# Counts loaded by twelves, rows fetched in 2 KB pieces, and nested fourth parts with jump hints in a two-layer mixture-of-experts kernel

## The chip, the cores and the metric

The kernel runs on one core of a Trainium2 chip. The metric is the device time of one execution in microseconds. Five engines work beside each other: TensorE (PE, with its weight loads as PEld), VectorE (DVE), ScalarE (ACT), GpSimd (POOL) and SyncE (SP). Here SP issues the transfers of weights, and POOL issues the gathers and scatters of token rows. Each engine runs its own instruction stream; semaphores order them. PE's stream also holds jumps, and loads of counts into its registers.

## The reference, cut to what matters

Two layers, each a token mixer and then a grouped top-2 mixture of 16 experts; layer 0 has 512 tokens (context and latent), layer 1 has 256. The part that the change touches:

```python
def moe_ffn(h, idx, w, w_gate, w_up, w_down):
    flat_e = idx.reshape(-1)
    order = jnp.argsort(flat_e)
    ...
    def expert_block(args):
        xb, ei = args
        return (jax.nn.silu(xb @ w_gate[ei]) * (xb @ w_up[ei])) @ w_down[ei]
    ...
    y = yb[dest] * w.reshape(-1)[order][:, None].astype(h.dtype)
    return jnp.zeros_like(h).at[tok].add(y)
```

`D_MODEL` is 1024, `D_EXPERT` 768. How many tokens go to an expert is known only at run time.

## The kernel before, in words

Each layer's expert stage (`moe`) goes through the 16 experts e in eight pairs p, with m = 0 or 1 for the expert of the pair. SP brings every weight once: four pieces `in_egu` (gate and up) and two `in_ed` (down) of 1536 KB for each expert, into a ring of slots that PE frees as it goes on (`wload`). A pair's tokens are gathered by POOL (`gather`, L1561, tile `xg`) and transposed on PE (`xt`).

An expert's tokens lie in a window of 128 (layer 0) or 96 (layer 1), cut in parts of 32. `hidden` computes gate and up for each part t into a PSUM tile `gu`, ACT and DVE make `sg` and `h` of it; `down` multiplies with the down weights into `dp`, with S = 0 for parts 0 and 1 and S = 1 for parts 2 and 3. A part's matmuls are 32 in gate and up and 24 in down; in f32 each of these is two weight loads and two matmuls on PE, so a part of gate and up is 128 instructions. In layer 0 parts 2 and 3, and in layer 1 parts 1 and 2, run only if the expert's count n exceeds 32 t: `when` (L1483) puts a run-time branch (L1487) around the part, and one matmul with a zero tile fills PSUM if it is left out. In layer 0 the third and the fourth part stand behind two branches, one after the other, in gate/up and in down.

The counts come from a tile `cnt` (`counts`, L1404): 16 of the experts, 8 maxima of the pairs, one overall. PE loads each into a register by itself (`count`, L1737): a TENSOR_LOAD and two check instructions, 31 times a layer. POOL loads those it needs in the same way (L1557, L1602).

In layer 0 the outputs of pairs 0 to 5 go by `scatter` to four planes in DRAM, a quarter of the columns each; S = 1 is sent only if the pair's maximum exceeds 64. A send is four indirect DMAs, one for each plane. After the last, `fetch(a)` brings half of the tokens back: 16 DMAs of 128 KB, then two POOL additions (L1615) of the two choices of each token. `collect` (tile `cl`) transposes the sum on PE and adds it to the result: half 0 at the end of expert 13, half 1 at the end of expert 14. The last two pairs are added by matmuls with one-hot tiles (`combine`, `cm`).

PE's expert matmuls keep the order in which the program writes them (`pin`); the work around them is placed by a scheduler.

## Time and profile before

| | |
|---|---|
| median of 3 runs | 1477.56 us (1477.24 to 1483.76) |
| profiled execution | 1479.13 us |
| its span in the trace | 1477.4 us |
| PE busy | 1250.3 us, 85% of the span |
| DVE, ACT, POOL busy | 682.2, 398.0, 140.8 us |
| DMA | 411.87 MB, mean 279 GB/s |
| mean granted clock of PE | 0.921 |

The page gives the mean over stages with different limits. Layer 0's expert stage lies from 391 to about 850 us, layer 1's from 1088 to about 1454. To read it, one takes the stages apart: where the DMA share is near one, the weights set the time; where PE is neither busy nor waiting for weights, its waits are to be looked up. "issue" in a wait means that nothing in the profile explains it; branches, register loads and checks are not counted as busy, and the waits that they cause appear in this way or under PEq, PE's sequencer.

### The profile page before, as it was taken

Reading aid. Unit: us, or ns where it says so; the run is one execution under the profiler, and the core shown is the slowest. Engines: PE = TensorE matmul, PEld = TensorE weight load, DVE = VectorE, ACT = ScalarE, POOL = GpSimd, SP = SyncE. Lnnn points to the kernel's source line nnn. Section 1 sums busy time; section 2 is a strip of 40 time slices with the busy share of each in tenths; the row PEclk is TensorE's granted clock in tenths of the full one; section 3 lists DMA queues with packets and bytes.
Section 4 is the critical chain, followed back from the end, with each engine's and each line's share of the span. In section 5 each row is a group of like instructions: output and inputs, shape, how many; then the busy total and the mean of one; then the engine's idle time right before and its main releaser. Section 6 shows DMA issues by size and latency. Waiting matters only on the chain. (4 is left out here: it accounts for less than half of the span.)

```text
span 1477.4 us, 27647 instructions
## 1 busy us (share of the span) xinstructions
PE 1250.3 (85%) x11433; PEld 726.9 (49%) x11434; DVE 682.2 (46%) x1773; ACT 398.0 (27%) x791; POOL 140.8 (10%) x153
## 2 busy tenths in 40 slices
PE   4999988898679799999878867998978688898774
PEld 0697553576334344554434435876833344454333
DVE  1847536876425111111123568737665245454445
ACT  2624234344110110111010134434431112121214
POOL 0000011102101111022133012002010000000000
PEclk8999999899799999999989988999989898998996
DMA  9421688134488998889998341273388999999981
GB/s 359 163 100 43 223 323 343 52 128 161 178 338 315 382 412 369 347 329 421 426 386 341 144 160 55 89 278 150 129 340 360 377 412 425 423 426 421 425 367 31
DMA packets 49475, 411.87 MB, mean 279 GB/s; under 512 B 7195, under 2 KB 11439, under 8 KB 18064
## 3 DMA queue, kind: packets, MB, share of 16 engines
q1 hardware_dynamic: 41200, 388.40, 64.6%
q0 software_dynamic: 7232, 17.71, 3.3%
q8 instruction: 140, 2.29, 0.6%
q10 hardware_dynamic: 864, 3.15, 0.5%
q14 instruction: 39, 0.32, 0.1%
HBM read 402.02 MB, written 13.11 MB: 281 GB/s over the span
## 5 line engine op out<-in xcount | busy, mean ns | idle before, releaser
L1665 DVE SCALAR_TENSOR_TENSOR h0p<-gu0p,gt0p,sg0p 128x192 f32<-128x192 f32 x64 | 25.3, 415 | 177.0 <-ACT sg0p L321 176.5
L345 PE MATMUL gu0p<-big,xe0p 128*32 128x384 f32 x992 | 91.8, 492 | 1.6 <-issue 1.4
L345 PE MATMUL gu1p<-more,big 128*32 128x384 f32 x976 | 85.5, 493 | 7.9 <-issue 3.0
L321 ACT ACTIVATE sg0p<-gu0p 128x192 f32<-128x192 f32 x64 | 19.6, 331 | 247.1 <-PE gu0p L345 243.8
L345 PE MATMUL gu0p<-ring,xe0p 128*32 128x384 f32 x768 | 74.8, 497 | 0.8 <-ACT sg0p L321 0.5
L345 PE MATMUL gu0p<-more,xe0p 128*32 128x384 f32 x800 | 74.7, 493 | 0.5 <-issue 0.5
L345 PE MATMUL ada<-ring,small 128*32 128x512 f32 x344 | 62.9, 684 | 14.2 <-DMA ring<-in_ada 14.2
L1665 DVE SCALAR_TENSOR_TENSOR h1p<-gu1p,gt1p,sg1p 128x192 f32<-128x192 f32 x48 | 19.9, 415 | 118.0 <-ACT sg1p L321 117.9
L345 PE MATMUL dp0p<-big,hT0p 128*32 128x256 f32 x792 | 59.4, 402 | 6.3 <-issue 4.0
L345 PEld LDWEIGHTS gu1p<-more,big 128*32 128x32 f32 x976 | 35.1, 111 | 51.3 <-issue 46.1
L345 PEld LDWEIGHTS gu0p<-big,xe0p 128*32 128x32 f32 x992 | 37.8, 111 | 45.4 <-issue 42.1
L321 ACT ACTIVATE y0p<-dp0p 64x512 f32<-64x512 f32 (+1 forms) x40 | 23.6, 591 | 132.9 <-PE dp0p L345 105.0
L321 ACT ACTIVATE y1p<-dp1p 64x512 fp32r<-64x512 f32 x64 | 37.9, 592 | 79.9 <-PE dp1p L345 79.1
L321 ACT ACTIVATE sg1p<-gu1p 128x192 f32<-128x192 f32 x48 | 15.9, 330 | 156.4 <-PE gu1p L345 141.0
L321 ACT ACTIVATE big<-big 128x512 f32<-128x512 f32 (+2 forms) x81 | 44.7, 575 | 48.8 <-DVE big L641 21.5
L1598 POOL DMA_INDIRECT plane<-y0p,to0p x36 | 35.6, 988 | 205.8 <-ACT y0p L321 180.0
L345 PE MATMUL zo<-zo,zw 128*128 128x256 f32 x384 | 54.7, 292 | 0.0
L345 PE MATMUL gu1p<-big 128*32 128x384 f32 x528 | 52.5, 510 | 0.0
L345 PE MATMUL dp0p<-ring,hT0p 128*32 128x256 f32 x624 | 48.9, 401 | 3.5 <-issue 3.2
L345 PEld LDWEIGHTS zo<-zo,zw 128*128 128x128 f32 x384 | 48.6, 191 | 6.6 <-issue 4.3
L345 PEld LDWEIGHTS <-zero 128*128 128x128 bf16 x105 | 10.0, 97 | 83.2 <-issue 64.8
L1730 DVE TENSOR_TENSOR y1p<-dp1p,y1p 64x512 fp32r<-64x512 f32 x64 | 44.0, 688 | 5.5 <-ACT y1p L321 3.9
(558 smaller groups left out, 2425.2 us busy)
## 6 DMA issues: line engine op xcount, KB each, us to landing
more<-in_egu SPq DMA_DIRECT2D x54, 1536.0 KB, 15.3
big<-in_egu SPq DMA_DIRECT2D x48, 1536.0 KB, 15.6
ring<-in_ada SPq DMA_DIRECT2D x27, 1536.0 KB, 8.0
ring<-in_ed SPq DMA_DIRECT2D x27, 1536.0 KB, 14.8
ring<-in_egu SPq DMA_DIRECT2D x26, 1536.0 KB, 13.5
big<-in_ed SPq DMA_DIRECT2D x21, 1536.0 KB, 12.9
more<-in_ed SPq DMA_DIRECT2D x16, 1536.0 KB, 10.7
ring<-in_odw SPq DMA_DIRECT2D x5, 1536.0 KB, 6.2
```

What stands on the lines that cost most here:

```text
L321: a = self.nc.scalar.activation(out, x, func, **kw)
L345: i = self.nc.tensor.matmul(out, lhsT, rhs, start=start, stop=stop, skip_group_check=True)
L1598: nc.gpsimd.indirect_dma_start(out=self.planes[q], out_offset=bass.IndirectOffsetOnAxis(ap=to[:, q, i, S:S + 1], axis=0), in_=Y[S][:, q // ...
L1665: nc.vector.scalar_tensor_tensor(H[:, t], p[:, 192:384], gt[:, 2 * m + t % 2, i, t // 2:t // 2 + 1], sg, op0=OP.mult, op1=OP.mult)
L1730: nc.vector.tensor_tensor(yl[r, q], dp[r], yh[r, q].bitcast(F32), op=OP.subtract)
```

## The change

`counts` puts the numbers of a pair and their maximum next to each other. PE loads twelve registers (four pairs) with one instruction, without checks, at the stage's start and again ahead of expert 6. There are two planes of twice the length instead of four: a plane holds half of the columns, a token's two quarters lie one behind the other, so a row index is 2 to + (q mod 2), and `fetch` brings four DMAs of 512 KB in pieces of 2 KB instead of sixteen of 128 KB. The scatters go in the order q = 0, 2, 1, 3, which alternates between the planes. Half 1 is collected in expert 15, behind its parts 0 and 1. Parts 2 and 3 of layer 0 (the third and the fourth) stand in one branch (n > 64), the fourth nested in the third behind a branch of its own (n > 96), and the PSUM tiles of both are taken ahead of it. A hint that the jump is likely taken stands in PE's stream some matmuls ahead of the branches on n > 64, for every expert. The diff, cut to its core:

```diff
     def open_planes(self, pool):
...
-        self.planes = [self.dram.tile([2 * T, 256], F32, name=f'plane{q}') for q in range(4)]
+        self.planes = [self.dram.tile([4 * T, 256], F32, name=f'plane{q}') for q in range(2)]
...
-        nc.vector.tensor_copy(cf[:, :NE], count)
...
+        c3 = cf[:, :3 * NP].rearrange('p (q x) -> p q x', x=3)
+        nc.vector.tensor_copy(c3[:, :, 0:2], count.rearrange('p (q m) -> p q m', m=2))
+        nc.vector.tensor_reduce(c3[:, :, 2], c3[:, :, 0:2], axis=AX.X, op=OP.max)
...
-        def when(rv, least, yes, no=None):
+        def when(rv, least, yes, no=None, label=None):
...
-            with tc.If(rv > least) as cmp:
+            with tc.If(rv > least, label=label) as cmp:
...
+        def hint(rv, label):
+            if rv is not None:
+                with tc.issue_after(self.last):
+                    tc.mark_branch_hint_location(label, hint=0, engines=[mybir.EngineType.PE])
...
-                        nc.vector.tensor_copy(to[r, q], tg[s, 2])
+                        nc.vector.tensor_scalar(to[r, q], tg[s, 2], 2.0, q % 2 * 1.0, op0=OP.mult, op1=OP.add)
...
-                for q in range(4):
-                    nc.gpsimd.indirect_dma_start(out=self.planes[q], out_offset=bass.IndirectOffsetOnAxis(ap=to[:, q, i, S:S + 1], axis=0),
+                for q in (0, 2, 1, 3):
+                    nc.gpsimd.indirect_dma_start(out=self.planes[q // 2], out_offset=bass.IndirectOffsetOnAxis(ap=to[:, q, i, S:S + 1], axis=0),
...
-                for i in range(2):
-                    for q in range(4):
-                        o = i * T + a * TC + j * 128
-                        nc.gpsimd.dma_start(rb[:, j, i, q * 256:(q + 1) * 256], self.planes[q][o:o + 128])
+                for q in range(2):
+                    o = a * TC + j * 128
+                    nc.gpsimd.dma_start(rb[:, j, :, q * 512:q * 512 + 512],
+                                        self.planes[q].rearrange('(i t c) d -> t i (c d)', i=2, c=2)[o:o + 128])
...
-            def part(t, j=range(4)):
-                p = self.ps(f'gu{l}{nm}{t}', 'pj' if m or t < 2 else 'b')
-                when(rv if t > l_first else None, 32 * t, lambda: [gu_mm(t, jj, p) for jj in j], lambda: z_mm(p, 384))
-                return p
...
+            def third():
+                part(2)
+                if nt > 3:
+                    when(rv, 96, lambda: part(3), lambda: zeros(3))
...
                     if j == 1:
+                        hint(rv, f'gu{l}{nm}')
                         middle()
...
             between()
+            p += [self.ps(f'gu{l}{nm}{t}', 'pj' if m else 'b') for t in range(2, nt)]
+            when(rv, 64, third, lambda: [zeros(t) for t in range(2, nt)], f'gu{l}{nm}')
             for t in range(2, nt):
-                swiglu(t, part(t))
+                swiglu(t, p[t])
...
+                def third():
+                    if nt > 3:
+                        when(rv, 96, lambda: d_mm(1), lambda: z_mm(dp, 512))
+                    else:
+                        z_mm(dp, 512)
+                    d_mm(0)
                 if S == 0:
+                    hint(rv, f'dp{l}{nm}')
...
-                    when(rv, 64, lambda: d_mm(0))
+                    when(rv, 64, third, lambda: z_mm(dp, 512), f'dp{l}{nm}')
...
+        def some_counts(e):
+            i = 3 * (e // 2)
+            _, n = nc.values_load_multi_w_load_instructions(cnt[0:1, i:i + 3 * NC // 2], engines=[mybir.EngineType.PE], min_val=0, max_val=T,
+                                                                skip_runtime_bounds_check_because='counts of T tokens, compared with constants only')
+            for p in range(NC // 2):
+                ns_[e + 2 * p], ns_[e + 2 * p + 1], ns_[NE + e // 2 + p] = n[3 * p:3 * p + 3]
+
         def count(i):
-            return nc.tensor.value_load(cnt[0:1, i:i + 1], min_val=0, max_val=T)
+            return ns_[i]
+        ns_, NC = {}, 8
...
         for e in range(NE):
             p, m = divmod(e, 2)
+            if e == NC - 2:
+                with tc.issue_after(self.last):
+                    some_counts(NC)
...
+                if ns and e == 2 * ns + 3:
+                    collect(got, 1)
...
-            if ns and 1 <= e - 2 * ns <= 2:
-                collect(got, e - 2 * ns - 1)
-                if e == 2 * ns + 1:
-                    got = fetch(1)
+            if ns and e == 2 * ns + 1:
+                collect(got, 0)
+                got = fetch(1)
```

PE before, an expert of layer 0 behind its parts 0 and 1 (the rows `gu0p_4346` and `gu0p_4347` are those two, `ISA x2` are the checks of a count):

```order
L1737 TENSOR_LOAD cnt_2917
L1737 ISA x2
L1737 TENSOR_LOAD cnt_2917
L1737 ISA x2
L1487 COMPARE_AND_BRANCH
L345 MATMUL gu0p_4421<-more_2060,xe0p_4183 32x384 x16
L345 MATMUL gu0p_4421<-big,xe0p_4183 32x384 x8
L345 MATMUL gu0p_4421<-ring,xe0p_4183 32x384 x8
L1487 UNCONDITIONAL_BRANCH
L345 LDWEIGHTS zero_2776
L345 MATMUL gu0p_4421<-zero_2776 128x384
L1487 UNCONDITIONAL_BRANCH
```

PE now, the same place (`gu0p_4929` and `gu0p_4930` are parts 0 and 1, `gu0p_5005` the third, `gu0p_5006` the fourth):

```order
L1874 BRANCH_PREFETCH_HINT
L345 MATMUL gu0p_4929<-ring,xe0p_4744 32x384 x8
L345 MATMUL gu0p_4930<-ring,xe0p_4744 32x384 x8
L1489 COMPARE_AND_BRANCH
L345 MATMUL gu0p_5005<-big,xe0p_4757 32x384
L1489 COMPARE_AND_BRANCH
L345 MATMUL gu0p_5006<-big,xe0p_4757 32x384 x8
L345 MATMUL gu0p_5006<-ring,xe0p_4757 32x384 x16
L345 MATMUL gu0p_5006<-big,xe0p_4757 32x384 x8
L1489 UNCONDITIONAL_BRANCH
L345 LDWEIGHTS zero_2772
L345 MATMUL gu0p_5006<-zero_2772 128x384
```

The loads between the matmuls are gone, a hint stands two groups of matmuls ahead, and the first jump now spans the third part with the branch of the fourth inside it.

POOL before, a send of a pair, with the gather of the pair after next (`xg`) behind S = 0; a DMASW semaphore is the landing of a DMA that POOL issued earlier:

```order
L1598 DMA plane_1413<-y0p_4199,to0p_3091 1024x256 [waits DMASW0_49,DMASW2_49,DVE_49,Activation_49]
L1598 DMA plane_1414<-y0p_4199,to0p_3091 1024x256 [waits DMASW3_49,DMASW1_49]
L1598 DMA plane_1411<-y0p_4199,to0p_3091 1024x256 [waits DMASW4_49,DVE_49]
L1598 DMA plane_1412<-y0p_4199,to0p_3091 1024x256 [waits DMASW7_49,DMASW5_49]
L1561 DMA xg_2061<-rows_2063,idx0p_3601 128x1024 [waits DMASW6_49,PE_49]
L1603 COMPARE_AND_BRANCH
L1598 DMA plane_1411<-y0p_4200,to0p_3091 1024x256 [waits DMASW2_49]
L1598 DMA plane_1412<-y0p_4200,to0p_3091 1024x256 [waits DMASW3_49]
```

POOL now, the same send:

```order
L1606 DMA plane_1412<-y0p_4160,to0p_3095 2048x256 [waits DMASW6_49,DMASW2_49,DMASW7_49,DVE_49,Activation_49]
L1606 DMA plane_1411<-y0p_4160,to0p_3095 2048x256 [waits DMASW3_49,DVE_49]
L1606 DMA plane_1412<-y0p_4160,to0p_3095 2048x256 [waits DMASW6_49]
L1606 DMA plane_1411<-y0p_4160,to0p_3095 2048x256 [waits DMASW7_49]
L1611 COMPARE_AND_BRANCH
L1606 DMA plane_1411<-y0p_4161,to0p_3095 2048x256 [waits DMASW1_49]
L1606 DMA plane_1412<-y0p_4161,to0p_3095 2048x256 [waits DMASW0_49]
L1606 DMA plane_1411<-y0p_4161,to0p_3095 2048x256 [waits DMASW4_49,DMASW2_49]
```

The third scatter waits for the landing of the first, since both write one plane, and the gather stands behind the second send instead of ahead of it.

PE before, the collect of half 1 between expert 14's down matmuls and expert 15's first gate and up matmuls:

```order
L345 MATMUL dp0p_7758<-big,hT0p_7641 32x256 x12
L350 MATMUL cl_7867<-const,rows_7564 128x128 x4
L350 MATMUL cl_7874<-const,rows_7564 128x128 x4
L350 MATMUL cl_7881<-const,rows_7564 128x128 x4
L350 MATMUL cl_7888<-const,rows_7564 128x128 x4
L345 MATMUL gu0p_7910<-big,xe0p_7394 32x384 x8
L345 MATMUL gu0p_7911<-big,xe0p_7394 32x384 x8
```

PE now, the end of expert 15's parts 0 and 1:

```order
L345 MATMUL gu0p_7683<-more_2056,xe0p_7228 32x384 x8
L345 MATMUL gu0p_7684<-more_2056,xe0p_7228 32x384 x8
L351 MATMUL cl_7759<-const,rows_7400 128x128 x4
L351 MATMUL cl_7766<-const,rows_7400 128x128 x4
L1489 COMPARE_AND_BRANCH
L345 MATMUL gu0p_7854<-big,xe0p_7241 32x384
```

The transposes of `cl` stand behind the two parts, ahead of the branch on the third. At the start of layer 0's expert stage POOL has eight single count loads ahead of its first gather, where it had four.

## Rows read from the trace of the kernel before

**Rows 1.** Stretches: length, busy PE, PEld, DVE, ACT, POOL, clock, DMA share, GB/s.

```profile
600.00:700.00 100.00, 95.50 (x1297) 48.32 (x1289) 15.78 (x28) 12.41 (x30) 17.42 (x18) 1.00 0.91 375
...
752.00:815.00 63.00, 48.37 (x536) 23.40 (x536) 19.58 (x40) 7.65 (x18) 20.66 (x26) 0.86 0.89 351
...
1088.00:1180.00 92.00, 70.04 (x718) 36.88 (x717) 40.74 (x199) 17.21 (x36) 2.12 (x2) 0.89 0.85 347
1180.00:1440.00 260.00, 218.77 (x2462) 108.41 (x2461) 120.42 (x411) 53.43 (x107) 5.94 (x6) 0.91 0.99 415
```

**Rows 2.** Waits of PE from 752 to 815: us in total, times, longest.

```profile
PE cl L350 <- POOL rows L1615: 13.0, 2, 8.2
```

**Rows 3.** Timeline of POOL from 733 to 800: start, length, instruction, idle before it.

```profile
733.84 0.98 POOL L1598 DMA_INDIRECT plane<-y0p,to0p  x1 [32.02 <-ACT y0p L321]
...
750.46 4.22 POOL L1613 DMA_DIRECT2D rows<-plane  x8 [0.95 <-DMA rows<-plane]
...
766.62 2.34 POOL L1615 TENSOR_TENSOR rows<-rows 128x1024 f32<-128x1024 f32 x1 [9.54 <-issue]
775.22 4.29 POOL L1613 DMA_DIRECT2D rows<-plane  x8 [6.25 <-PE cl L350]
```

**Rows 4.** Timeline of PE from 752 to 815.

```profile
769.01 2.61 PE L350 MATMUL cl<-const,rows 128*128 128x128 f32 x11 [8.21 <-POOL rows L1615]
...
798.90 3.46 PE L350 MATMUL cl<-const,rows 128*128 128x128 f32 x15 [4.76 <-POOL rows L1615]
802.29 6.40 PE L345 MATMUL gu0p<-big,xe0p 128*32 128x384 f32 x64
```

**Rows 5.** Line L1598 (scatter) from 730 to 770.

```profile
DMA to landing us min/median/max: 6.6/7.5/7.8
```

**Rows 6.** Waits of PE from 391 to 752.

```profile
PE gu0p L345 <- issue: 10.2, 7, 5.0
PE xt0p L350 <- DMA xg<-rows,idx0p: 6.0, 1, 6.0
PE gu0p L345 <- DVE h0p L1665: 4.9, 6, 1.1
```

**Rows 7.** Line L1487 (jumps), 391 to 856: durations ns min/median/max.

```profile
L1487 PEldq COMPARE_BRANCH  x98: 65/208/5807, 393.1 to 847.0; - x98
```

**Rows 8.** Reads of the zero tile from 391 to 856, same columns.

```profile
L345 PE MATMUL gu0p<-zero x24: 322/336/501, 402.3 to 816.0; 128*128 128x384 bf16 x24
L345 PE MATMUL dp0p<-zero x14: 376/390/391, 429.5 to 833.3; 128*128 128x512 bf16 x14
```

**Rows 9.** Timeline of PE around jumps and count loads.

```profile
441.25 0.50 PE L345 MATMUL gu0p<-zero 128*128 128x384 bf16 x1 [5.01 <-issue]
...
486.77 0.59 PE L345 MATMUL xt0p<-zero 128*128 128x512 bf16 x2 [1.46 <-ACT sg0p L321]
...
508.77 0.34 PE L345 MATMUL gu0p<-zero 128*128 128x384 bf16 x1 [0.90 <-issue]
511.07 0.50 PE L345 MATMUL gu0p<-zero 128*128 128x384 bf16 x1 [1.96 <-issue]
...
677.78 0.38 PE L345 MATMUL dp0p<-zero 128*128 128x512 bf16 x1 [1.71 <-issue]
```

**Rows 10.** Line L1737 (count loads) on PE from 440 to 860.

```profile
L1737 PEldq TENSOR_LOAD <-cnt x15: 297/300/319, 485.0 to 507.8; - x15
```

**Rows 11.** Line L1557 (count loads of POOL), and the timeline from 380.

```profile
L1557 POOLq TENSOR_LOAD <-cnt x15: 281/289/830, 382.4 to 1099.7; - x15
...
386.68 1.14 POOL L1561 DMA_INDIRECT xg<-rows,idx0p  x1 [14.29 <-DVE sp0p L1535]
```

**Rows 12.** Stretches in which the DMA engines stand in layer 1.

```profile
1100.50:1106.00 5.50, 5.50 (x46) 1.73 (x49) 5.03 (x40) 2.37 (x3) 0.00 (x0) 1.00 0.06 19
1124.50:1127.50 3.00, 2.35 (x31) 1.74 (x24) 0.91 (x3) 0.66 (x2) 0.00 (x0) 1.00 0.00 0
```

**Rows 13.** DMA issues of SP from 735 to 815.

```profile
751.90 0.33 SPq L338 DMA_DIRECT2D ring<-in_ed  x1
```

More of the change, by code (lines that the diff above doesn't have):

```diff
@@ L345, in mm @@
         i = self.nc.tensor.matmul(out, lhsT, rhs, start=start, stop=stop, skip_group_check=True)
+        self.last = i.ins
         if self.pin:
@@ L1681, in hidden @@
                     if j == 1:
+                        hint(rv, f'gu{l}{nm}')
                         middle()
@@ L1748, in gathers @@
             for S in range(2):
-                gather(info[p][0][0], info[p][1], S, NE + p)
+                gather(info[p][0][0], info[p][1], S, p)
         xe, G0 = [], []
@@ L1800, in experts @@
                         got = fetch(0)
-            if ns and 1 <= e - 2 * ns <= 2:
-                collect(got, e - 2 * ns - 1)
-                if e == 2 * ns + 1:
-                    got = fetch(1)
-            last, was = [f'p{p}{m}', m, (f'p{p}{m}', H), rv], (tok, ti, full, to, i, NE + p)
+            if ns and e == 2 * ns + 1:
+                collect(got, 0)
+                got = fetch(1)
+            last, was = [f'p{p}{m}', m, (f'p{p}{m}', H), rv], (tok, ti, full, to, i, p)
             if e == 1 and l == 0:
@@ L1814, in experts @@
             self.pin = pin
-        most = nc.values_load(cnt[0:1, NE + NP:NE + NP + 1], min_val=0, max_val=T)
+        most = nc.values_load(cnt[0:1, 3 * NP:3 * NP + 1], min_val=0, max_val=T)
         with tc.If(most > WIN[l]):
```

44 lines of the change are left out of this document (22 added, 22 removed).

## The prediction

> **What bounds the kernel now.** I read the span by stages first, in the table of stretches [rows 1]: it gives for each the busy time of TensorE (PE) and the share of the DMA engines. It shows three regimes. In layer 0's expert stage before 752 us both are nearly full: in 600 to 700, PE is busy 95.50 of 100 us and the DMA share is 0.91. There the weights and the matmuls wait for each other in turn, so a microsecond taken off PE returns in part. From 752 to 815 PE is busy for only 48.37 of 63 us. In layer 1 from 1180 to 1440 the DMA share is 0.99: the weights set the time there, and nothing that PE gains can show before the last of them lands.
>
> The waits of PE in 752 to 815 name what is late: 13.0 us in two waits for the POOL additions of L1615 [rows 2]. PE's timeline puts them at 769.01 (8.21 us) and 798.90 (4.76 us) [rows 4]. The weights were not late there: the second wait stands ahead of matmuls that then run without one, at 802.29. So these 13.0 us are the largest single item that a change in this code can take, and they lie on the path to layer 0's end. The other PE gaps of this stage are smaller and scattered: jumps over skipped thirds and fourths (L1487), and the count loads (L1737).
>
> **The change part by part.** *Fetch and collect.* POOL's timeline [rows 3] shows the chain: the four scatters of the last pair start at 733.84, one behind the other; sixteen fetch DMAs go out in two eights, the second from 750.46 over 4.22 us; the second addition starts at 766.62, so its data were late, not POOL. SP had issued 1536 KB weight pieces at 751.90 and after [rows 13], level with the second eight, and shares the engines with it.
>
> Now the third scatter writes the plane of the first and waits for its landing, 7.5 us in the median [rows 5]. It goes out near 733.8 + 7.5 = 741.3, the fourth near 742.6, and they land near 750. Four fetches are issued then, at the 0.53 us of one of the eight (4.22 / 8), so by about 752.5: 2 us before the last of the sixteen, and ahead of or level with SP's burst rather than behind it. The bytes are the same 2 MB. Lower end: they get through before the burst, the additions (2.34 us) end by 760.5, and 8.21 us vanish. Upper end: they share with the burst as before, and 8.21 remain. I take the half, 4.2 gained.
>
> The second collect moves from the end of expert 14 to behind the first two parts of expert 15. Before, its chain took from the fetch at 775.22 to PE's start at 798.90, 23.7 us; it starts now about 4 us earlier and has four issues instead of sixteen, while PE comes to it later by those two parts (the 64 rows from 802.29, half of them, alone are 6.40 us [rows 4]). So it is ready with some 10 us in hand, and 4.76 us go. Sum: -9.0, ends -4.8 and -13.0. What is late next is PE itself.
>
> *Counts on PE.* A single load is 0.300 us in the median [rows 10], with two check rows behind it, and 31 a layer become two loads of twelve. The trace exposes 1.46 us at 486.77 and 0.90 at 508.77 behind such loads [rows 9]; all of PE's waits that nothing in the profile explains ahead of gate/up matmuls are 10.2 us, 7.0 of which are two jumps (below) [rows 6], so the loads cost 2.4 to 4.7 us; I take 3.5. The first twelve loads cost nothing, since PE waited 6.0 us for the first gathered rows beside them [rows 6]. What one load of twelve costs no row shows: 0.30 if it is one access, 3.6 if it is twelve. The first stands directly behind PE's first gate/up matmul, the second behind 36 queued down matmuls, which hide a part. I take 2.0 and 1.0, so -0.5 net; ends -4.4 and +4.8.
>
> [...]
>
> *Counts on POOL.* POOL still loads singly, and eight such loads stand ahead of the first gather now, four before. One is 0.289 us plus its two checks, so four add 1.2 us and up to about twice that; the gather of before started at 386.68, held by VectorE [rows 11], and that wait hides a part. PE waits for this gather, so what is left counts in full: I take 0.9 (ends 0 and 2.4). Both count parts together: +0.4.
>
> *Jumps.* The zero fills of layer 0 say how often they are taken [rows 8]: 14 experts fill the down result (no fourth part), so 2 run it; 24 gate/up fills leave 10 experts that skip the third part as well. These 10 skip 256 instructions in one jump now, where they took two jumps over 128, and 192 where it was twice 96 in the down part: 20 long jumps. A jump is 0.208 us in the median but 5.807 at worst [rows 7], and the worst stood between two zero fills, exactly where the second jump goes: PE idled 5.01 us at 441.25; 1.96 at 511.07 is the same place of another expert, 1.71 at 677.78 a down part [rows 9]. That is 8.7 us; with smaller ones of 0.3 to 0.5 us I count 10 for layer 0. No row shows a hint at work in this place, so it is bounded: all 10 returned, or none with more lost (a rival). I take half, -5, since some of it only turns into waiting for weights. Against it stands that the PSUM tiles of both parts are taken ahead of the jump: in six places PE already waits for VectorE's h0p (4.9 us [rows 6]) ahead of the third part, and will wait for the second h0p too, some 0.4 us each, +2.5. Net -2.5; ends -10 and +8.
>
> *Scatters earlier in layer 0.* The same landing wait holds POOL some 6 us more for each send, and for a pair with over 64 rows the next gather now stands behind both sends. Gathers are issued while the pair before still runs, and PE waited for gathered rows only once, at the start [rows 6], so I cost this at nothing; if that cover went, it would be some 6 us for each such pair.
>
> *Layer 1.* Loads and jumps go there too, but only in 1088 to 1180 does the DMA share (0.85) leave room [rows 1]. In 1124.5 to 1127.5 it is 0.00 with PE busy 2.35 of 3 us [rows 12]: such holes, where SP waits for slots that PE has yet to free, are all that can return. In the longest, 1100.5 to 1106, PE is full, so only work ahead of it could shorten it. I take -2; ends 0 and -6, of the 8.5 us of the two.
>
> **Sum.** -9.0 + 0.4 - 2.5 - 2 = -13.1 us. The profiled execution was 1479.1 us (span 1477.4), 1.6 above the median of 1477.6 that the measurement will use; the terms are differences, so from the median the forecast is 1464.5.
>
> **The rivals.** *The first wait stays and the hints do nothing.* POOL's serial scatters put the fetches level with SP's burst, and the jumps still miss. For it: the 7.5 us landing [rows 5] is certain, and the margin over the burst is under 2 us. Then only 4.8 us of the second wait and a little else go: about 1473, within the bound of no change.
>
> *The long jumps miss.* Place: the 20 long jumps of layer 0, PE-bound before 752. [...] Price: if each exposed the 1.96 us of 511.07, 39 us come in and the 10 of today go: 1477.6 - 9 + 0.4 + 2.5 - 2 + 29 = 1498.5. It decides from about 1.0 us per long jump above what I assumed ((13.1 + 7.4) / 20). Against it: before, two jumps skipped the same code, with a matmul between, and only some missed.
>
> [...]
>
> *More comes back.* Both POOL waits vanish (-13), jumps and loads return all (-10, -4), and layer 1's holes close (-6), less 3.4 for the gather and the second h0p: about 1448. For it: the items are all real idle time of PE; against it: before 752 the DMA share is 0.9.
>
> **How the numbers follow.** Forecast (1457 to 1470): 0.45. More comes back (1444 to 1457): 0.21. First wait stays (1470 to 1481): 0.23. Long jumps miss: 0.11, part of it still under 1485. The bound of 0.5% (7.4 us) is about what a measurement of this kernel tells from no change, so faster means under 1470.2, slower over 1485: 0.66, 0.25, 0.09. The range 1448 to 1481 leaves out the far ends of both outer cases.
>
> **What would show it.** Right: no wait of PE for the POOL additions at the second collect, at most 4 us at the first; POOL's third scatter idle for some 6 us behind the first's landing; no PE gap of 5 us between zero fills in layer 0; TENSOR_LOAD on PE in four rows in all; layer 1's 1180 to 1440 unchanged at a DMA share of 0.99. Wrong: COMPARE_BRANCH rows of 1 us and more at many of the long jumps, a load of twelve well over 3.6 us, or a first collect as late as before.

## The result, and the profile after

The changed kernel takes 1494.51 us in the median of 8 runs (1490.74 to 1499.29), beside 1479.09 us of the kernel before: the ratio is 1.0095 with a 95% interval of 1.0077 to 1.0114. It is slower, by about 14 us. The forecast was 1464.5 with a range of 1448 to 1481: wrong in sign, and outside the range.

In the differences of ratios below, 0.001 is 1.48 us; a difference of two such ratios is good to about 4 us.

**Where the time came in.** The first PE row of layer 1's preparation (tile `adat`) is a landmark: what stands before it is layer 0. PE's timeline of the kernel before, then of the kernel after (start, length, instruction, idle before it):

```profile
855.60 0.65 PE L350 MATMUL adat<-const,adarow 128*128 128x128 f32 x4 [0.72 <-ACT adarow L435]
```

```profile
872.40 0.66 PE L351 MATMUL adat<-const,adarow 128*128 128x128 f32 x4 [0.68 <-ACT adarow L436]
```

Layer 0 ends 16.8 us later. From there to the end of the span it was 1477.4 - 855.6 = 621.8 us and is 1493.3 - 872.4 = 620.9. All that was lost was lost in layer 0. The stretch of layer 1 in the kernel after answers [rows 1]: the weights set the time there as before, at a DMA share of one.

```profile
1180.00:1440.00 260.00, 213.10 (x2376) 99.75 (x2380) 115.80 (x396) 53.25 (x106) 5.92 (x6) 0.89 1.01 425
```

**First place: the lists.** Among shorter stretches of layer 0 in the same view, one stands out. Of the kernel before:

```profile
445.00:470.00 25.00, 25.00 (x290) 12.93 (x286) 10.88 (x19) 1.80 (x5) 0.00 (x0) 0.98 0.90 371
```

Of the kernel after:

```profile
445.00:470.00 25.00, 15.58 (x74) 12.03 (x71) 11.52 (x31) 0.59 (x1) 1.00 (x1) 0.50 0.53 223
```

PE was busy 25.00 of 25 us with 290 matmuls, and is busy 15.58 with 74; the granted clock fell from 0.98 to 0.50, and the DMA share from 0.90 to 0.53. PE's timeline of the kernel after says with what:

```profile
445.92 1.02 PE L345 MATMUL sl0p<-aux,G0p 128*128 128x10 f32 x4
448.52 1.02 PE L345 MATMUL sl0p<-aux,G0p 128*128 128x10 f32 x4 [1.58 <-DVE G0p L1521]
...
466.52 1.02 PE L345 MATMUL sl0p<-aux,G0p 128*128 128x10 f32 x4 [0.78 <-DVE G0p L1521]
467.47 4.71 PE L345 MATMUL gu0p<-ring,xe0p 128*32 128x384 f32 x32
```

Twelve groups of four small matmuls (`sl0p`, the token lists of pairs 2 to 7; each group reads a tile `G0p` that DVE makes just ahead of it) stand in one block. Eleven of them wait for DVE, 1.58 + 10 x 0.78 = 9.4 us, and the gate/up matmuls behind them start at a low clock: 4.71 us for the 32 of 467.47, at 0.58 from 467.5 to 472.2, where 32 take 2.76 us at 1.00 (the row at 706.78 below). Nothing in the diff names these lists. The order of instructions shows how they moved. PE before, in this place (rows of the order, not of the trace):

```
L345 MATMUL sl0p_3528<-aux_2778,G0p_3529 128x10 x4
L345 MATMUL gu0p_3705<-ring,xe0p_3392 32x384 x7
L345 MATMUL gu0p_3706<-ring,xe0p_3392 32x384 x8
L345 MATMUL gu0p_3705<-more_2060,xe0p_3392 32x384
L345 MATMUL sl0p_3528<-aux_2778,G0p_3535 128x10 x4
L345 MATMUL gu0p_3705<-more_2060,xe0p_3392 32x384 x7
```

PE now:

```
L345 MATMUL dp0p_3412<-big,hT0p_3263 32x256 x15
L345 MATMUL sl0p_3519<-aux_2774,G0p_3520 128x10 x4
L345 MATMUL sl0p_3519<-aux_2774,G0p_3526 128x10 x4
L345 MATMUL sl0p_3519<-aux_2774,G0p_3532 128x10 x4
```

`mm` ties each matmul of an expert behind whatever was written on PE just before it. Before, that was a count load, which is itself tied to nothing, so expert 2's gate/up matmuls could be placed between the lists, and while DVE made the next `G0p`, PE had work. Now the count loads of expert 2 are gone, and its first matmul is tied behind the last list.

**Second place: the fetch.** POOL's timeline of the kernel after, which answers [rows 3]:

```profile
744.83 0.99 POOL L1606 DMA_INDIRECT plane<-y0p,to0p  x1 [16.85 <-ACT y0p L321]
...
751.23 0.98 POOL L1606 DMA_INDIRECT plane<-y0p,to0p  x1 [4.11 <-DMA plane<-y0p,to0p]
753.70 0.98 POOL L1606 DMA_INDIRECT plane<-y0p,to0p  x1 [1.49 <-DMA plane<-y0p,to0p]
760.16 2.99 POOL L1620 DMA_DIRECT2D rows<-plane  x4 [5.48 <-DMA plane<-y0p,to0p]
776.11 2.33 POOL L1623 TENSOR_TENSOR rows<-rows 128x1024 f32<-128x1024 f32 x1 [12.96 <-DMA rows<-plane]
786.19 2.34 POOL L1623 TENSOR_TENSOR rows<-rows 128x1024 f32<-128x1024 f32 x1 [7.75 <-DMA rows<-plane]
```

SP's DMA issues in the kernel after, which answer [rows 13] (1536 KB each):

```profile
757.45 0.33 SPq L338 DMA_DIRECT2D ring<-in_ed  x1
758.74 0.33 SPq L338 DMA_DIRECT2D big<-in_ed  x1
760.03 1.62 SPq L338 DMA_DIRECT2D big<-in_egu  x2
767.91 0.33 SPq L338 DMA_DIRECT2D ring<-in_egu  x1
771.16 0.33 SPq L338 DMA_DIRECT2D more<-in_egu  x1
```

And PE's timeline of the kernel after at the collect, which answers [rows 4]:

```profile
778.49 0.47 PE L351 MATMUL cl<-const,rows 128*128 128x128 f32 x1 [7.39 <-POOL rows L1623]
788.58 2.61 PE L351 MATMUL cl<-const,rows 128*128 128x128 f32 x11 [9.61 <-POOL rows L1623]
```

The third and the fourth scatter now wait for the landing of an earlier one, and the four fetches go out from 760.16, in the midst of a burst of six weight pieces. 2 MB of rows share the engines with 9 MB of weights, at a DMA share of 1.01 from 757.45 to 786.19, and the second addition starts 26 us after the first fetch was issued. PE waits 7.39 + 9.61 = 17.0 us for the first collect, where it waited 13.0 for both [rows 2]. At the second collect (828.34 and after) it waits for no addition, as was forecast.

**The smaller things.** Lines of the loads and the hint in the kernel after (durations ns min/median/max):

```profile
L1760 PEldq TENSOR_LOAD <-cnt x4: 850/871/1030, 398.5 to 1236.6; - x4
```

```profile
L1874 PEldq BRANCH_PREFETCH_HINT  x53: 31/31/50, 422.8 to 1454.2; - x53
```

Waits of PE from 391 to 756 in the kernel after, which answer [rows 6] (us in total, times, longest):

```profile
PE dp0p L345 <- issue: 15.0, 6, 3.7
PE sl0p L345 <- DVE G0p L1521: 10.2, 12, 1.6
PE xt0p L351 <- DMA xg<-rows,idx0p: 9.0, 1, 9.0
PE gu0p L345 <- issue: 7.2, 3, 3.7
```

A load of twelve takes 0.87 us. The waits that nothing explains, where the jumps show, are 15.0 + 7.2 = 22.2 us; before, up to 752, they were 11.6 (for `dp0p`) + 10.2 [rows 6] = 21.8. The wait for the first gathered rows grew from 6.0 to 9.0 us.

### The profile page after: what moved, and what is told of

Same layout as the page of the kernel before. It is cut to its first block, busy times and chain, and to the rows that moved or that the text cites. A ratio compares the mean times of both kernels' runs of the same rounds, so it can differ in the third digit from the quotient of the medians.

```text
span 1493.3 us, 27443 instructions
## 1 busy us (share of the span) xinstructions
PE 1245.8 (83%) x11433; PEld 738.3 (49%) x11434; DVE 683.0 (46%) x1773; ACT 398.9 (27%) x791; POOL 127.4 (9%) x127
## 5 line engine op out<-in xcount | busy, mean ns | idle before, releaser
L345 PE MATMUL gu0p<-ring,xe0p 128*32 128x384 f32 x768 | 80.8, 515 | 0.0
L345 PE MATMUL gu0p<-more,xe0p 128*32 128x384 f32 x800 | 71.6, 486 | 0.0
L345 PEld LDWEIGHTS gu0p<-big,xe0p 128*32 128x32 f32 x992 | 44.9, 110 | 36.4 <-issue 25.8
L345 PE MATMUL gu1p<-big 128*32 128x384 f32 x528 | 57.0, 548 | 3.8 <-DMA big<-in_egu 2.8
```

Source lines behind the costliest of these rows:

```text
L345: i = self.nc.tensor.matmul(out, lhsT, rhs, start=start, stop=stop, skip_group_check=True)
```

## The experiments

Every kernel below computes everything. Names beginning with a are the kernel after with something undone, with b the kernel before with something of the change done alone; c, d and e are combinations.

**Is it the lists?** a_spread takes away only the tie between the last list and expert 2's first gate/up matmul; the rest of the change stays.

```diff
-        if self.pin:
+        if self.pin and not self.loose:
             self.tc.keep_in_program_order(i)
+        self.loose = False
...
             W = load_gu(e)
+            self.loose = l == 0 and e == 2
```

> The changed kernel, but expert 2's first gate/up matmul of layer 0 is not pinned behind the token lists of pairs 2 to 7, so that the list matmuls can lie between the expert matmuls again, as they did before the change. Theory (removing the single count loads removed the breaks in PE's pinned order, and the twelve list matmul groups became one block, in which PE idled 9.4 us in eleven waits for G0p): about 9 us below the changed kernel's 1494.5, so 1484 to 1488, and no row of 0.78 us waits between 446 and 466. Rival (the weights set the time there and PE's waits in the block cost nothing): 1492 to 1496.

Measured: 1478.11 us, ratio 1.0003 (0.9985 to 1.0021), 13.6 us less than the kernel after. The stretch of a_spread:

```profile
445.00:470.00 25.00, 25.00 (x240) 12.15 (x239) 9.60 (x16) 1.81 (x5) 0.00 (x0) 0.86 1.01 428
```

PE's timeline of a_spread, two lists with expert 2's work between:

```profile
455.52 0.61 PE L347 MATMUL sl0p<-aux,G0p 128*128 128x10 f32 x4
456.06 1.50 PE L347 MATMUL gu0p<-more,xe0p 128*32 128x384 f32 x16
457.48 0.61 PE L347 MATMUL sl0p<-aux,G0p 128*128 128x10 f32 x4
```

All list groups but the first cost 0.61 us instead of 1.02 with 0.78 of waiting. The gain is 4 us more than the 9.4 us of waits, which fits the lists in the block and the matmuls behind them running at the granted clocks of 0.50 and 0.58 read above. b_block is the counterpart, the kernel before with the lists forced into one block:

```diff
+            if self.block is not None:
+                self.tc.add_manual_dep(i.ins, self.block.name, NOSYNC)
```

> The kernel before with one edit to the order alone: expert 2's matmuls in layer 0 are queued behind the twelve list groups, so that these stand in one block as in the changed kernel; every load, jump and DMA stays. Theory (the block is the main cause of the loss: 9.4 us of waits for G0p, some 5 us more for the same list matmuls and what follows at half the granted clock): 10 to 14 us more, 1.007 to 1.0095 of before, with a granted clock near 0.5 in the block. Rival (the lists only cost together with the changed loads and hints): 0.998 to 1.003.

Measured: 1489.42 us, 1.0072 (1.0050 to 1.0093), 10.6 us lost by the order alone. Its stretch:

```profile
445.00:470.00 25.00, 15.14 (x110) 12.12 (x106) 9.89 (x18) 0.59 (x1) 0.00 (x0) 0.64 0.33 129
```

So the block costs 10.6 to 13.6 us, shown from both sides. Of what the change lost against the kernel before, it is the largest part.

**Is it the first gather?** a_gate issues POOL's count loads behind the first gather.

```diff
+        def after_gate(load):
+            if l:
+                return load()
+            with tc.issue_after(self.gate):
+                return load()
```

> The changed kernel, but POOL's count loads are issued behind the first gather of layer 0 instead of ahead of it. Theory (eight single loads hold the gather, and PE waits for it): the gather starts at least 3 us earlier against the end of the router's work, and the time is 2 to 5 us below 1494.5, so 1489.5 to 1492.5. Rival (the gather was held by VectorE's list entries all the same): no change, 1494 to 1495.

Measured: 1489.47 us, 1.0086 (1.0060 to 1.0112). PE's wait for the first gather is 5.9 us again instead of 9.0; the time is 1.3 us less, less than can be told apart.

**Is it the planes, the hints or the nesting?** a_nohint leaves out the hints, a_flat_nohint the nesting as well; a_planes goes back to four planes, their scatter order and sixteen fetches.

```diff
-            if rv is not None:
+            if False:
                 with tc.issue_after(self.last):
                     tc.mark_branch_hint_location(label, hint=0, engines=[mybir.EngineType.PE])
```

> The changed kernel without the jump hints; the nested branches stay. In the changed kernel PE idled 19.7 us in layer 0 behind jumps, 10 us more than before. [...] Theory B (the hints themselves disturb the fetch of instructions): 8 to 12 us less, 1483 to 1487. Theory C (the hints help a little, and without them it is worse): 1498 to 1505.

Measured: 1487.46 us, 1.0066 (1.0045 to 1.0088). The gain is some 4 us, with intervals that overlap. It can't be put down to the hints, since without them the order of the lists changes as well: ten of the twelve groups stand between down matmuls again. That order alone brings expert 2 nothing, since its gate/up matmuls stand behind the last list, whose last matmul starts at 468.3 there and at 467.2 in the kernel after. Where the 4 us come from stays open.

> The changed kernel without hints and with the third and fourth part behind two branches again, as before the change. Without hints alone it measured 1.0066 of before. Theory (one jump over 256 instructions misses more often than two over 128): layer 0's jump rows of 1 us and more fall from 34 to 44 us to about 31, and the time falls by another 4 to 8 us, to 0.999 to 1.004 of before. [...]

Measured: 1492.65 us, 1.0074 (1.0047 to 1.0101): the nesting is not what made the kernel slower. Its trace holds something else, the fetch and the burst. POOL's first fetch in a_flat_nohint, SP's first weight piece of the burst, and the waits of PE from 740 to 870:

```profile
759.79 3.00 POOL L1620 DMA_DIRECT2D rows<-plane  x4 [6.08 <-DMA plane<-y0p,to0p]
```

```profile
760.68 0.33 SPq L338 DMA_DIRECT2D ring<-in_ed  x1
```

```profile
PE cl L351 <- POOL rows L1623: 14.7, 2, 9.6
```

Here the fetch goes out 0.9 us ahead of the burst, as the prediction wanted it, and PE still waits 14.7 us for the rows.

```diff
-        self.planes = [self.dram.tile([4 * T, 256], F32, name=f'plane{q}') for q in range(2)]
+        self.planes = [self.dram.tile([2 * T, 256], F32, name=f'plane{q}') for q in range(4)]
```

> The changed kernel with four planes, the scatter order and the sixteen fetches of 128 KB of before; the later collect of half 1 stays. Theory (a third scatter that waits for the first's landing delays the fetch behind SP's weights; the changed kernel waits 17.0 us for the POOL additions at the first collect): the wait falls to 6 to 9 us, and the time to 1484 to 1488. Rival (the wait is set by SP's weights ahead of the fetches, whatever the pieces): within 3 us of 1494.5.

Measured: 1485.85 us, 1.0066 (1.0043 to 1.0089), 4.3 us less with overlapping intervals. The waits for the collect did not go: waits of PE from 740 to 860 in a_planes:

```profile
PE cl L351 <- POOL rows L1623: 18.2, 2, 11.7
```

In its trace the first fetch goes out 10.5 us after the first scatter (748.29 - 737.80) instead of 15.3, and the wait is no shorter. So serial scatters are not why the rows are late. c1_three_undone undoes hints, block and late gather at once and keeps the loads of twelve, the planes, the nesting and the moved collect.

> The changed kernel with three things undone: no hints, the lists between the expert matmuls again, and the first gather ahead of POOL's count loads. The nested branches, the loads of twelve, the two planes and the later collect stay. Alone these three gave about -14, -4 and -2 us against the changed kernel. If they add up: 1494.5 - 20 = 1474 to 1477 (0.996 to 0.998 of before). If the weights absorb part (they hold PE before 752): 1478 to 1482, no faster than the list alone undone.

Measured: 1478.99 us, 0.9988 (0.9973 to 1.0003). With the side effects taken off, the change is 1.8 us faster than before, which can't be told from nothing. Its waits for the collect are still 16.4 us.

**Why does the collect's wait not go?** b_move moves only the second collect into expert 15; b_late moves both one expert later.

```diff
+                if ns and e == 2 * ns + 3:
+                    collect(got, 1)
...
-            if ns and 1 <= e - 2 * ns <= 2:
-                collect(got, e - 2 * ns - 1)
-                if e == 2 * ns + 1:
-                    got = fetch(1)
+            if ns and e == 2 * ns + 1:
+                collect(got, 0)
+                got = fetch(1)
```

> The kernel before with one edit: half 1 is collected in expert 15 behind its parts 0 and 1 rather than at the end of expert 14. Theory of the prediction (the second wait of 4.76 us for the POOL addition goes and nothing takes its place): 3.5 to 5 us less than before, 0.9965 to 0.9977. Rival (the transposes and additions later in the layer lengthen its end by as much): 0.999 to 1.002.

Measured: 1480.53 us, 0.9991 (0.9977 to 1.0005). Waits of PE from 740 to 860 in b_move:

```profile
PE cl L350 <- POOL rows L1615: 11.5, 1, 11.5
```

The second wait is gone, and the first is 11.5 where it was 8.2. The moved collect stands behind the first one and can't have lengthened it by itself: in the trace of b_block, which leaves fetch and collect as they were, the two waits are 11.2 and 1.3 us.

> The kernel before with both collects moved by one expert: half 0 in expert 14 behind its parts 0 and 1, half 1 in expert 15 at the same place. PE then comes to each when the POOL additions have been over. Theory (the 13.0 us of waits lie on the path to layer 0's end and what follows is PE-bound): 10 to 13 us less, 0.991 to 0.993 of before. Rival (the fetch of half 1 collides with weights, or the later additions on VectorE become the end of the layer): 0.995 to 1.000.

Measured: 1479.89 us, 0.9982 (0.9963 to 1.0001). The same view of b_late:

```profile
PE cl L350 <- POOL rows L1615: 11.9, 2, 10.3
```

Now the second is the long one. In these traces the sum of the two changes little, from 13.0 to 12.5, 11.5 and 11.9 us; where the collect stands decides how it is shared out. The next runs ask whether what holds the rows is the weights of expert 13 and after, which SP issues as soon as slots come free. d1_hold is c1_three_undone with one more wait: the first of those weight pieces waits until the first fetch has landed. Behind it on SP's queue stand only further weights.

```diff
+        if self.behind is not None:
+            self.tc.add_manual_dep(d.ins, self.behind.name, SYNC)
+            self.behind = None
...
+            if ns and e == 2 * ns + 2:
+                self.behind = self.fetched
```

> The changed kernel with hints, list order and gather order undone as in c1 (0.9988 of before), and one wait added: SP holds the weights of expert 13's down step until the first fetch of rows has landed. Theory (PE's 16 to 17 us of waits at the first collect come from SP's 1536 KB pieces that go ahead of the fetch, and these weights are not needed before some 785 us): the waits fall to 0 to 5 us and the time by 10 to 14 us, 0.989 to 0.992. Rival (held weights are late for PE instead, in expert 14 or 15): 0.996 to 1.002, with waits on DMA there.

Measured: 1461.73 us, 0.9899 (0.9875 to 0.9923), 13.2 us less than c1_three_undone. POOL's timeline of d1_hold:

```profile
735.51 0.99 POOL L1620 DMA_INDIRECT plane<-y0p,to0p  x1 [23.22 <-ACT y0p L321]
...
749.20 2.99 POOL L1634 DMA_DIRECT2D rows<-plane  x4 [4.56 <-DMA plane<-y0p,to0p]
755.42 2.37 POOL L1639 TENSOR_TENSOR rows<-rows 128x1024 f32<-128x1024 f32 x1 [3.23 <-DMA rows<-plane]
758.12 2.38 POOL L1639 TENSOR_TENSOR rows<-rows 128x1024 f32<-128x1024 f32 x1 [0.34 <-DMA rows<-plane]
```

SP's timeline of d1_hold, the first of the held pieces:

```profile
758.04 0.33 SPq L338 DMA_DIRECT2D ring<-in_ed  x1
```

The second addition starts 8.9 us after the first fetch was issued, not 26. Counted from the first scatter, the weights go out 22.5 us after it (758.04 - 735.51), where it was 12.6 in the kernel after, and PE doesn't miss them: among its waits from 755 to 843 none is for weights. d2_hold puts the hold into the kernel before, with the moved collect and eight fetches of 256 KB.

> The kernel before with half 1 collected in expert 15, the fetch in eight DMAs of 256 KB from four planes, and the same hold of SP's weights behind the first fetch. Counts, jumps and lists are those of before. Theory: both waits for the POOL additions (13.0 us) go, 10 to 13 us less, 0.991 to 0.993. Rival (as in the two earlier moves of the collect, which gave 0.999 and 0.998, the wait turns up elsewhere): 0.996 to 1.000.

Measured: 1467.93 us, 0.9934 (0.9913 to 0.9956): the hold works there too. a_hold is the kernel after with the hold alone, the block of lists left as it is.

> The changed kernel with one edit: SP holds the weights of expert 13's down step until the first fetch of rows has landed. Hints, the block of lists and POOL's count loads ahead of the gather stay. Theory (of the changed kernel's time 17 us are PE's waits for rows whose fetch stands behind SP's weights): 10 to 15 us less than 1494.5, 0.999 to 1.003 of before. Rival: the gain came with the other three edits only, 1.005 to 1.010.

Measured: 1479.67 us, 0.9999 (0.9982 to 1.0015), 14.2 us less than the kernel after. Waits of PE from 740 to 860 in a_hold:

```profile
PE cl L356 <- POOL rows L1630: 4.5, 2, 2.3
```

Of the 17.0 us of waiting 12.5 are gone, and the time followed. The three edits add up within the error: 13.6 (block) + 14.2 (hold) + 1.3 (gather) = 29.1 us. e_hints below is the kernel after with exactly these three and lies 0.0219 or 32.4 us under it; d1_hold, without the hints too, 0.0196 or 29.0.

**What are the parts worth once the way is clear?** From d1_hold: e_hints puts the hints back, e_flat takes the nesting out, e_single loads the counts singly.

> The kernel d1 (0.9899 of before) with the hints of the changed kernel put back; the branches are nested in both, lists, gather and hold as in d1, so nothing but the hints differs. Hints on the flat branches cost the kernel before 3.5%. Theory A (a hint costs wherever it stands, through more and longer waits for instructions): 15 to 50 us more, 1.000 to 1.02, jump rows of 1 us and more summing to 40 us or more in either layer. Theory B (nested, the hinted jump comes next after its hint, and the loss needs an unhinted jump between hint and target, as the flat form has it): within 4 us of d1, 0.988 to 0.993.

Measured: 1462.49 us, 0.9876 (0.9847 to 0.9905): in this form the hints cost nothing and bring nothing that can be told. The idle time of PE directly behind jumps that took 1 us or more, added up over layer 0 from the trace, is about 20 us in e_hints and about 11 in d1_hold, yet layer 0 ends at 842.06 and 842.76. One pair of traces doesn't put the difference down to the hints: the same sum runs from 13.5 (a_planes) to 21.7 us (a_spread) in the traces with nested branches and hints, and from 10.9 (c1_three_undone) to 19.7 us (e_single, below) in those with nested branches and none.

> The kernel d1 with the third and fourth parts behind two branches again, without hints. Theory (the one long jump misses more than two short ones, the rival on record): 3 to 8 us less than d1, 0.984 to 0.988. Rival (nesting saves a little, since layer 1's jump rows sum to 20 us nested and to 29 flat): 0 to 5 us more, 0.990 to 0.994.

Measured: 1467.41 us, 0.9923 (0.9895 to 0.9950): the nesting may bring 3.5 us; the intervals overlap.

```diff
-            return ns_[i]
+            c = 3 * (i // 2) + i % 2 if i < NE else 3 * (i - NE) + 2
+            return nc.tensor.value_load(cnt[0:1, c:c + 1], min_val=0, max_val=T)
```

> The kernel d1 with PE's counts loaded one by one again (with their checks), everything else as in d1. Theory (the single loads expose 2.4 to 4.7 us in layer 0, and layer 1 has no use for the rest; a load of twelve took 0.87 us): 2 to 5 us more than d1, 0.991 to 0.9935. Rival (PE waits for weights there anyway): 0.989 to 0.991.

Measured: 1475.15 us, 0.9973 (0.9955 to 0.9990): the loads of twelve are worth 10.9 us here. PE's timeline of e_single behind a run of such loads:

```profile
505.42 2.79 PE L352 MATMUL gu0p<-more,xe0p 128*32 128x384 f32 x32 [0.76 <-issue]
```

Layer 0's expert stage up to the landmark, first of d1_hold and then of e_single:

```profile
391.00:842.76 451.76, 401.48 (x4822) 198.69 (x4823) 114.61 (x302) 61.78 (x138) 61.18 (x58) 0.96 0.86 352
```

```profile
391.00:852.92 461.92, 409.73 (x4823) 198.95 (x4823) 115.92 (x313) 61.31 (x138) 61.22 (x58) 0.95 0.85 345
```

Of the 10.2 us by which the stage is longer, PE is idle for 1.9 and busy for 8.3, with the same matmuls. So the gaps behind the loads hardly grew in sum, and why the same matmuls take longer isn't shown. Nor do the parts simply add: with single loads and flat branches d2_hold has 0.9934, better than e_single's 0.9973 with single loads and nested ones (d2_hold differs in the planes too, which by the next two runs don't matter). Next to flat branches single loads cost little: e_flat has 0.9923, d2_hold 0.9934. Why they cost more beside nested ones stays open.

b_hint puts the hints alone into the kernel before, beside single loads and flat branches.

```diff
+                 when(rv if t > l_first else None, 32 * t, ..., f'gu{l}{nm}' if t == 2 else None)
...
+                hint(rv, f'gu{l}{nm}')
```

> The kernel before with the hints of the changed kernel added at its branches on n > 64, nothing nested; the lists stay between the expert matmuls. In the kernels with hints the rows of 1 us and more behind jumps summed to 39 to 44 us in layer 0 and 39 to 40 in layer 1; without hints to 25 to 34 and 20 to 31. Theory A (the hints disturb the fetch): sums near 40 in both layers, and 1 to 5 us more, 1.0005 to 1.0035. Theory B (the long sums came from the nested jumps): sums of 25 to 31 as before, and 0.999 to 1.001.

Measured: 1527.72 us, 1.0348 (1.0316 to 1.0379), 51 us slower. In b_hint the landmark stands at 877.17, 21.6 us later than before, and the other half is lost in layer 1. Waits of PE from 1110 to 1490 in b_hint:

```profile
PE dp1p L345 <- issue: 27.9, 7, 9.7
PE gu1p L345 <- issue: 18.0, 9, 5.0
PE gu1p L345 <- PEq L1488: 6.8, 8, 2.0
```

In the kernel before these were 13.1 (dp1p), 14.8 (gu1p, nothing that explains it) and 3.2 us (gu1p, PE's sequencer). A hint row itself is 0.035 us in the median of 54, so it isn't their own time. Much of the loss lies behind the jumps: the idle time behind those of 1 us and more in layer 0 is about 30 us, where it was about 12 before. Layer 1's branches are flat in e_hints too, where layer 1 took no longer than before (620.7 us from the landmark, 621.8 before), so the flat form alone doesn't explain it. It stays open whether the single loads or the place of the code do.

The last two runs ask whether two planes cost anything once the weights are held: e_p8 is d1_hold with four planes and eight fetches of 256 KB, e_p16 with the sixteen of before.

> The kernel of d1_hold (lists interleaved, first gather early, no hints, SP's weights held behind the landing of the first fetch), with four planes again, so that no scatter waits for the landing of another, and a fetch of eight DMAs of 256 KB. d1_hold measured 0.9899 of before. Theory (the serial scatters of two planes hold POOL some 7 us in each send and delay gathers and the fetch): 0.985 to 0.987, the fetch out some 6 us earlier than in d1_hold. Rival (with the weights held behind the fetch, the planes no longer matter; what a_planes gained was the changed phase of the weights): 0.988 to 0.992.

Measured: 1463.86 us, 0.9897 (0.9862 to 0.9932).

> As e_p8, with the sixteen DMAs of 128 KB of before as the fetch. Theory (four planes are worth 4 to 6 us and four issues against sixteen some 4 us of POOL's time): 0.987 to 0.990. Rival (the number of DMAs in a fetch does not matter once the weights are held behind it): the same as e_p8 within 0.002.

Measured: 1468.18 us, 0.9907 (0.9879 to 0.9934). POOL's timeline of e_p8, the first scatter, the first fetch and the second addition:

```profile
739.53 0.99 POOL L1620 DMA_INDIRECT plane<-y0p,to0p  x1 [29.34 <-ACT y0p L321]
...
751.56 0.79 POOL L1634 DMA_DIRECT2D rows<-plane  x1 [7.18 <-DMA plane<-y0p,to0p]
...
761.67 2.38 POOL L1639 TENSOR_TENSOR rows<-rows 128x1024 f32<-128x1024 f32 x1 [0.69 <-DMA rows<-plane]
```

Both are equal to d1_hold within their intervals. From the first scatter (739.53 in e_p8, 735.51 in d1_hold) to the second addition (761.67, 758.12) it is 22.1 us with four planes and 22.6 with two. The shape of the transfers, on which the prediction spent its working, decides nothing that can be told once the weights are held. What the 4.3 us of a_planes were, noise included, stays open.

The fastest of all are e_hints at 0.9876, e_p8 at 0.9897 and d1_hold at 0.9899, which can't be told apart. All three beat both kernels. What separates e_hints from the change is the order of the lists, the hold, and the place of POOL's count loads.

## Why the prediction was wrong, point by point

**What bounds the kernel: right.** The 13.0 us of waits for POOL's additions lie on the path. When the hold took 12.5 us of such waits out of the kernel after, 14.2 us came back; d2_hold, made from the kernel before, has none of them left and is 9.8 us faster than it.

**Fetch and collect, -9.0: the step that failed first.** The terms of the issue were about right. The third scatter came 6.4 us after the first (7.5 assumed), the fetch 15.3 us after it (16 assumed: 733.8 to 750). What failed is "ahead of or level with SP's burst rather than behind it", in two ways.

First, it compared the new fetch with the burst of the old trace, 18.1 us after the first scatter [rows 3, 13], as if it stood still. SP issues a piece when PE frees a slot (from 730 to 800 all its waits in the kernel after are for PE: 21.0 us for down and 17.0 for gate/up matmuls). In the kernel after, the burst came 12.6 us after the first scatter (757.45 - 744.83), the fetch shared the engines with all of it, and the wait grew from 13.0 to 17.0. The nested branches, a part of the same change, are what brought the burst forward. In the unheld kernels with flat branches it comes 16.6 to 18.3 us after the first scatter, in the six with nested ones (the kernel after, a_spread, a_gate, a_nohint, a_planes, c1_three_undone) 12.3 to 12.6. PE's timeline of the kernel before, then of the kernel after, just ahead of the burst at 751.90 and 757.45:

```profile
751.54 0.32 PE L345 MATMUL gu0p<-zero 128*128 128x384 bf16 x1 [1.12 <-ACT xe0p L321]
```

```profile
755.65 0.32 PE L345 MATMUL gu0p<-zero 128*128 128x384 bf16 x1 [0.58 <-DVE h0p L1673]
...
756.90 0.50 PE L345 MATMUL gu0p<-ring,xe0p 128*32 128x384 f32 x3
```

Before, the piece goes out as the zero fill of the fourth part ends, some 6 us after the third part's last read of `ring`. Now the fill stands inside the third part, and the piece goes out as that last read ends.

Second, being ahead of the burst is not enough: in a_flat_nohint the fetch goes out 0.9 us ahead of it, and the wait is 14.7 us. Without the hold, the kernels with the changed expert stage wait 14.7 (a_flat_nohint) to 19.7 us (a_spread) for the collect, where it was 13.0. So the term was 2 to 7 us of waiting more, not 9 us less. The upper end, -4.8, took the second wait for gone at no price to the first; b_move and b_late show the sum of the two nearly unchanged, and d1_hold that it belongs to the rows behind the weights. The rival "the first wait stays" had this mechanism, but left the wait at the 8.2 us of before.

**The order of the lists: missing from the sum.** The prediction has the count loads by their time alone. That they also left the gate/up matmuls of the next expert untied on PE, and that the lists were spread among these for this reason, has no term in the prediction, though the order of both kernels shows it in a dozen rows. It cost 13.6 us by a_spread (10.6 by b_block), about as much as the whole forecast gain.

**Counts on PE, -0.5: too small on both sides.** A load of twelve is 0.87 us, not the 2.0 and 1.0 us assumed; 0.87 / 12 is 0.073 us for each register. The value of the loads removed was taken from the gaps that the trace puts down to them, 3.5 us; with the way clear e_single gives 10.9, most of it as PE's busy time and not in gaps. The end of -4.4 was too tight. **On POOL, +0.9:** the wait grew by 3.0 us, more than the bound of 2.4; undoing it gave back 1.3 us, which can't be told from nothing.

**Jumps, -2.5: the mechanism failed, the cost was small.** The gap of 5.01 us at 441.25 is 3.71 at 442.76, and others came. The idle time directly behind jumps of 1 us and more in layer 0, added up as above, went from about 12 to about 20 us, though layer 0's expert stage runs 78 such branches instead of 98. PE's timeline of the kernel after:

```profile
442.76 0.50 PE L345 MATMUL gu0p<-zero 128*128 128x384 bf16 x2 [3.71 <-issue]
...
555.22 0.39 PE L345 MATMUL dp0p<-zero 128*128 128x512 bf16 x1 [3.68 <-issue]
...
706.78 2.76 PE L345 MATMUL gu0p<-big,xe0p 128*32 128x384 f32 x32
```

The forecast had let half of these waits vanish by the hints. No run shows a hint that shortens a jump, or what makes one jump long and another short; nor does one show that a jump over 256 instructions costs more than two over 128 (0.9899 in d1_hold, 0.9923 in e_flat). In time the rise shows as nothing: up to 756 the unexplained waits are 22.2 us beside 21.8, and e_hints isn't slower than d1_hold. The rival of the long jumps gave 1498.5, near the time that came, but by a loss that no run shows: its 20 long jumps were to lose 1.96 us each, 39 us, and with spread lists and the hold the same jumps stand in the fastest kernel. That the two times lie so near is chance.

**Scatters, 0: right as far as shown.** PE waited for gathered rows only once in layer 0 again, at the start, and two planes or four make no difference that can be told once the weights are held (e_p8, e_p16).

**Layer 1, -2: within its ends.** It is 0.9 us shorter from the landmark to the end (0 to 6 were given).

**The sum.** Without the fetch the forecast was 0.4 - 2.5 - 2 = -4.1 us. c1_three_undone, with 3.4 us more waiting for the collect than before, is 1.8 us faster, so its other parts made about -5.2 (an estimate from these two numbers). The kernel after is then c1_three_undone's -1.8, plus 13.6 for the block and 1.3 for the gather, 13.1 us; the 1 us to the measured 14 lies within the error. Between the forecast of -13.1 and the measured +14 lie 27 us: 13.0 are the fetch, forecast at -9.0 and with 4.0 us more waiting instead, and 13.6 the block (an estimate, which takes a microsecond of that waiting for one of time). What made the prediction wrong is one wait that grew instead of going, and one order that changed where the diff doesn't point.

## What to carry to other kernels

A transfer that is late because it shares the engines with prefetched weights was not helped here by issuing it with fewer instructions (four instead of sixteen, 17.0 us of waiting instead of 13.0), by asking for it 0.9 us ahead of them (14.7) or by using it later (11.9). What helped was to hold the prefetch, by a wait of the first weight piece on the transfer's landing (4.5 in a_hold); the weights had the microseconds to spare. When a forecast sets two transfers against each other in time, ask what the rest of the change does to either: a branch of another shape freed the weights' slot some 5 us earlier (12.3 to 12.6 us after the first scatter instead of 16.6 to 18.3). Where code is tied in program order on an engine, an instruction that is removed may have been the place at which other work could slip in; compare the whole order of that engine before and after, not only the places of the diff. The gaps behind a register load are no bound for what its removal brings: 3.5 us were read from them and 10.9 came in one form of the kernel, next to nothing that can be told in another.

## What the runs showed of the hardware that was not expected

- PE's granted clock was 0.50 in a stretch of 25 us in which it ran groups of four small matmuls between waits of 0.78 us (0.98 before, when it was busy throughout). A list matmul took 0.36 us there in the median, 0.25 in the kernel before, so beside the waits the work itself was slower.
- Twelve registers in one load took 0.87 us, one takes 0.30 [rows 10].
- A branch hint is 0.03 us (31 ns in the median of 53), and yet hints alone made the kernel before 3.5% slower, while they left d1_hold's time as it was (0.9876 and 0.9899). The runs don't tell what makes the difference.
- 2 MB of rows took 8.9 us from first issue to the second addition in d1_hold, where the next weight piece was issued 8.8 us after that first issue, and 26 us in the kernel after, beside six weight pieces of 1536 KB.
